# Strassen products of a hybrid encoder step: A21 and A22 of the next job loaded ahead of A12, low parts issued behind the eviction, S3 behind the second product's low part

## The chip, the cores and the metric

The kernel runs on one core of one Trainium2 chip. The metric is the device time of one launch in microseconds, the median of three runs; a profiled execution of the same program gives the trace that is read here.

## The reference, cut to what matters

One step of an encoder layer over 576 frames (512 of a prompt, 64 of a running stream), model width 2048, inner width 5504, all in fp32:

```python
h = x + jnp.concatenate([oa, ob], axis=-1) @ w_out        # oa: attention heads, ob: gated MLP groups
n = rms_norm(h, g)
a, gv = jnp.split(n @ w_up, 2, axis=-1)
ac, new_prev = causal_dwconv(prev, a, cw, cb)
y = h + (jax.nn.silu(ac) * gv) @ w_down
```

What goes before (RMS norm, the products of w_in, chunked attention, spatial gating) takes the first 609 us of the span and is not touched by the change.

## The kernel before

Each fp32 product is made of three products in a rounded type. A weight tile w is split into hi (a rounded copy) and lo = w - hi, and so is the activation, into u0 and u1. TensorE then adds hi x u0, hi x u1 and lo x u0 in one PSUM bank. The hi part of a tile is a cast on ScalarE (L216), the lo part a subtraction on VectorE (L217); both are made by `split_raw`. All weights come from DRAM through the helper `load_raw` (L206), whose transfers are issued by SyncE (SP in the profile).

From w_out on the products are done by 2x2 blocks with seven products in place of eight (Strassen in Winograd's form). The program is a list of jobs: 12 jobs of the out product (o0 to o11), 40 of the up product (u3 to u42) and 29 of the down product (d0 to d28). A job has a pair of output tiles and a window of units; a unit is a 256-row piece of the contraction. All up jobs have 8 units. Out jobs have 1 to 8 and down jobs 1 to 8, since their contraction is cut into visits: near the ends of both stages the windows are short and change from job to job.

A job needs four weight blocks A11, A12, A21 and A22, of one 128x128 tile per unit each (512 KB at 8 units). On VectorE the sums S1 = A21 + A22 (L875), S3 = A11 - A21 (L878, into A21's buffer), S2 = S1 - A11 (L879, into A11's) and T = A12 - S2 (L882, into A12's) are made of them. The seven products go in the order 1, 2, 6, 5, 7, 3, 4; their weights are A11, A12, S2, S1, S3, T and A22. Their results are added in three PSUM banks: x takes products 1, 6, 7 and 4, one after another, y product 2, z products 5 and 3. So product 6 must not start before product 1 has been evicted from x. The activation sums (units un_c, un_n, un_f) are made beside, in the out and down stages by VectorE and ScalarE while the jobs run (`form`).

The main loop, for product i of the whole list, does `prep(i + 1)` (sums, split and the loads for the next job), `mm(i)`, `evict(i - 1)`, `finish(i - 3)` and `form`. The tool that builds the program orders the instructions of each engine anew, by its own model of when each is ready; the orders shown below are those that it gave. The pool of weight buffers (tag raw) has five: four blocks and S1. A block of the next job takes the buffer that was given back first, and its transfer waits on SP until the lo part that last read the buffer is done. In the kernel before the next job's A11 takes the old A11's buffer, A12 the one of S1 (free behind lo_5), A21 that of A21 (behind lo_7), A22 that of A12 (behind lo_3), and the new S1 that of A22.

The matmuls are at L909 (hi x u0), L911 (hi x u1) and L913 (lo x u0), the evictions of out and down jobs at L979 (one addition into the residual tiles r0, r1, or y), those of up jobs at L940 to L962. Residual tiles are loaded at L865, and stored at L985 and L694. The activations of the up product go to DRAM at L999 (ac) and come back as fa and fb (L791) for the down product's units (L543, L546, L567, L568).

Of the kernel before, what the change touches and what calls it, by code (L numbers as in the profile page):

```python
# [9 lines left out]
F32R = mybir.dt.float32r  # L10
AF = mybir.ActivationFunctionType
ALU = mybir.AluOpType
# [3 lines left out]
P = 128  # L16
# [109 lines left out]
def layer(ctx: ExitStack, tc: tile.TileContext, xT, xg0, wst, cst, strip, ckT, cv, gws, cstate,  # L126
          yT, kTo, vTo, convo, gvo, stream):
    nc = tc.nc
    const = ctx.enter_context(tc.tile_pool(name="const", bufs=1))
    wpool = ctx.enter_context(tc.tile_pool(name="wpool", bufs=3))  # L130
# [32 lines left out]
    def big(name):  # L163
        return tmpp.tile([P, 640], F32, tag="tmp", name=name)
# [30 lines left out]
    def f(ap):  # L195
        return ap.bitcast(F32)
# [3 lines left out]
    def load_raw(keys, name):  # L200
        raw = wpool.tile([P, 8 * P], F32, tag="raw", name=f"raw_{name}", bufs=5)
        w = len(keys) * P
        src = wst[woff[0]:woff[0] + P * w].rearrange("(p c) -> p c", p=P)
        woff[0] += P * w
        stream.append(keys)
        nc.sync.dma_start(raw[:, :w], src)  # L206
        return raw

    def split_raw(raw, n, name, fast=False):
        hi = wpool.tile([P, 8 * P], F32R, tag="hi", name=f"hi_{name}", bufs=2)  # L210
        lo = wpool.tile([P, 8 * P], F32R, tag="lo", name=f"lo_{name}", bufs=2)
        w = n * P
        if fast:
            nc.vector.tensor_copy(hi[:, :w], raw[:, :w])
        else:
            nc.scalar.copy(hi[:, :w], raw[:, :w])  # L216
        nc.vector.tensor_tensor(lo[:, :w], raw[:, :w], f(hi[:, :w]), ALU.subtract)  # L217
        return hi, lo
# [612 lines left out]
    def strassen(jobs):  # L831


        work = [(job, r) for job in jobs for r in ORDER]
        R, PSX, EV, HL, RES = {}, {}, {}, {}, {}
        tt = nc.vector.tensor_tensor

        def window(job):
            return range(HP) if job[0] == UP else range(*PLANS[job[0]][job[1]][1:3])

        def single(job):

            return job[0] == DOWN and PLAN[job[1]][1] == 0

        def extra(job, r):
            return 1 if single(job) and r in (2, 3, 4) else 0

        def load(job, q):
            mi, half = int(q[0]) - 1, int(q[1]) - 1
            if job[0] == UP:  # L850
                keys = [(("ag"[mi], job[1]), 2 * i + half) for i in window(job)]
            else:
                m = (job[0], 2 * PLANS[job[0]][job[1]][0] + mi)
                keys = [(m, 2 * p + half + (job[0] == DOWN)) for p in window(job)]
                if single(job) and half:
                    keys.append((m, 0))
            R[job, q] = load_raw(keys, f"{job[0]}{job[1]}_{q}")

        def load_res(job):
            if job[0] != UP:  # L860
                i, lo = PLANS[job[0]][job[1]][:2]
                RES[job] = [big(f"r{c}_{job[0]}{job[1]}")[:, :T] for c in range(2)]
                first, later = (hs, ys) if job[0] == DOWN else (xT, hs)
                for c in range(2):
                    nc.sync.dma_start(RES[job][c], (later if lo else first)[2 * i + c])  # L865

        def prep(i):
            if i >= len(work):
                return
            job, r = work[i]  # L870
            name = f"{job[0]}{job[1]}"
            w = len(window(job)) * P
            if r == 2:
                R[job, "s1"] = wpool.tile([P, 8 * P], F32, tag="raw", name=f"s1_{name}", bufs=5)
                tt(R[job, "s1"][:, :w], R[job, "21"][:, :w], R[job, "22"][:, :w], ALU.add)  # L875
            elif r == 6:
                a11, a21 = R[job, "11"][:, :w], R[job, "21"][:, :w]
                tt(a21, a11, a21, ALU.subtract)  # L878
                tt(a11, R[job, "s1"][:, :w], a11, ALU.subtract)  # L879
            elif r == 5:  # L880
                a12 = R[job, "12"][:, :w]
                tt(a12, a12, R[job, "11"][:, :w], ALU.subtract)  # L882
            q = {1: "11", 2: "12", 6: "11", 5: "s1", 7: "21", 3: "12", 4: "22"}[r]
            HL[job, r] = split_raw(R[job, q], len(window(job)) + extra(job, r), f"{r}_{name}")
            nxt = {5: "11", 7: "12", 3: "21", 4: "22"}.get(r)
            at = i // len(ORDER) + 1
            if nxt and at < len(jobs):
                load(jobs[at], nxt)
                if r == 4:
                    load_res(jobs[at])  # L890

        def operand(job, k, r):
            return UN[UNITS[job[0]], k, r][0]
# [42 lines left out]
        def evict_up(j, r, ps):  # L936
            x, y, z = ps
            if r == 1:
                EV[j] = {"cc": big(f"cc_{j}")[:, :T]}
                nc.scalar.copy(EV[j]["cc"][:, LEFT], x)  # L940
            ev = EV[j]
            if r == 2:
                ev["e"] = e = conv_edges(j)
                tt(e[:, 2:2 + HF], y, ev["cc"][:, LEFT], ALU.add)
            elif r == 6:
                nc.scalar.copy(ev["cc"][:, RIGHT], x)
            elif r == 5:
                ev["act"] = big(f"act_{j}")[:, :T]
                nc.scalar.copy(ev["act"][:, RIGHT], z)
            elif r == 7:  # L950
                tt(ev["act"][:, RIGHT], x, ev["act"][:, RIGHT], ALU.add)
            elif r == 3:
                e, cc, m = ev["e"], ev["cc"], SEQ - HF
                tt(e[:, 2 + HF:514], z[:, :m], cc[:, HF:SEQ], ALU.add)  # L954
                tt(e[:, 516:580], z[:, m:], cc[:, SEQ:], ALU.add)
                ev["t"] = conv(j, e)
            elif r == 4:
                t, act = ev["t"], ev["act"]
                nc.scalar.activation(t, t, AF.Silu)
                tt(act[:, HF:SEQ], act[:, HF:SEQ], t[:, HF:SEQ], ALU.mult)  # L960
                tt(act[:, SEQ:], act[:, SEQ:], t[:, 514:578], ALU.mult)
                tt(act[:, :HF], x, t[:, :HF], ALU.mult)  # L962

        def evict_sum(job, r, ps):
            x, y, z = ps[:3]
            rs = RES[job]
            i, _, hi, _ = PLANS[job[0]][job[1]]
            src, m, c = {1: (x, 0, LEFT), 2: (y, 0, LEFT), 6: (x, 0, RIGHT), 5: (z, 1, RIGHT),
                         7: (x, 1, RIGHT), 3: (z, 0, RIGHT), 4: (x, 1, LEFT)}[r]
            dst = rs[m]  # L970
            end = job[0] == OUT and hi == HP
            if end and r in (2, 3, 7, 4):
                k = 2 * i + m
                if Y[k] is None:
                    Y[k], Y_SLOT[k] = slot([P, T], F32, f"y_{k}")
                dst = Y[k]
            if r == 4 and len(ps) == 4:
                tt(rs[1][:, RIGHT], ps[3], rs[1][:, RIGHT], ALU.add)
            tt(dst[:, c], src, rs[m][:, c], ALU.add)  # L979
            if r in (3, 4):  # L980
                if end:
                    out_done(2 * i + m)
                else:
                    out = hs if job[0] == OUT else yT if hi == NP else ys
                    nc.sync.dma_start(out[2 * i + m], rs[m])  # L985

        def evict(i):
            if 0 <= i < len(work):
                job, r = work[i]
                if job[0] == UP:  # L990
                    evict_up(job[1], r, PSX[job])
                else:
                    evict_sum(job, r, PSX[job])

        def finish(i):
            if 0 <= i < len(work):
                job, r = work[i]
                if r == 4 and job[0] == UP:
                    nc.sync.dma_start(acs[job[1]], EV.pop(job[1])["act"])  # L999
                    if job[1] == NF - 1:  # L1000
                        nc.sync.dma_start(convo, conv_new)
# [10 lines left out]
        def form(job):  # L1012
            return limit(job) and advance(step, forming, limit(job))

        for q in ("11", "12", "21", "22"):
            load(jobs[0], q)
        load_res(jobs[0])
        prep(0)
        for i in range(len(work)):
            prep(i + 1)  # L1020
            mm(i)
            evict(i - 1)
            finish(i - 3)
            form(work[i][0])
            if work[i][1] == ORDER[-1]:
                while form(work[i][0]):
                    pass
        evict(len(work) - 1)

    flush()  # L1030
    banks(misc=8)
    strassen([(OUT, v) for v in range(len(PLAN_O))])
    for _ in rms_scale(rx, "h"):
        pass
# [91 lines left out]
```

## Time and profile before

| | |
|---|---|
| median of three runs | 2320.21 us (2320.01 to 2320.77) |
| the profiled execution | 2321.35 us |
| its span, first to last instruction | 2319.6 us |
| TensorE busy | 2250.9 us, 97%, 16768 matmuls |
| VectorE busy | 1694.7 us, 73% |
| ScalarE busy | 1003.5 us, 43% |
| GpSimd busy | 207.8 us, 9% |
| DRAM traffic | 286 MB, 123 GB/s |

TensorE is in the rows as PE, its weight loads as PEld, VectorE as DVE, ScalarE as ACT, GpSimd as POOL and SyncE's queue as SPq. A row of the trace with a bracket at its end gives the idle time of the engine ahead of the instruction and what ended it. Names of tiles are given without the job's number: x_o is the x bank of an out job, hi_d the hi part of a down job. The stages in the trace: heads and gated MLP to 609 us, out jobs to 816, norm and the first up products to 915, up jobs to 1803, down jobs to 2320.

### The profile page before, as it was taken

What the parts mean: (1) busy time and instruction counts of PE and PEld (TensorE: products, weight loads), DVE (VectorE), ACT (ScalarE), POOL (GpSimd) and SP (SyncE); (2) the same over time, 40 slices, a digit from 0 to 9 for tenths busy, and PEclk for the clock granted to TensorE, in tenths of its full rate; (3) what the DMA queues carried; (4) which work ended last, traced back from release to release, by engine and by line L of the source; (5) the groups of instructions that cost most, each with busy time, mean ns of one, the idle gap of its engine ahead of it and who ended that gap; (6) DMA issues with size and microseconds to landing.
All of it is one profiled execution on the core that took longest, in us unless ns stands there. A gap on an engine that the chain in (4) does not pass through costs nothing.

```text
span 2319.6 us, 41325 instructions
## 1 busy us (share of the span) xinstructions
PE 2250.9 (97%) x16768; PEld 2233.3 (96%) x16768; DVE 1694.7 (73%) x2605; ACT 1003.5 (43%) x1485; POOL 207.8 (9%) x242
## 2 busy tenths in 40 slices
PE   7999999999999889999999999999999899999988
PEld 7999999999999779999999999999999899999988
DVE  7645655654787669777777777677777999978767
ACT  5444444432433345444444444444445444434332
POOL 4000000000002102111111111111111000000000
PEclk9999999999999889999999999999999999999999
DMA  6322222222344332333332333323333665545444
GB/s 211 102 92 92 97 94 80 83 84 78 119 152 138 127 103 92 103 125 105 104 117 93 123 106 103 120 91 122 107 102 123 210 195 173 188 161 179 157 146 141
DMA packets 107391, 286.24 MB, mean 123 GB/s; under 512 B 12096, under 2 KB 20416, under 8 KB 107200
## 3 DMA queue, kind: packets, MB, share of 16 engines
q1 hardware_dynamic: 107200, 283.60, 37.2%
q8 instruction: 132, 2.16, 0.4%
q14 instruction: 59, 0.48, 0.1%
HBM read 241.62 MB, written 41.93 MB: 122 GB/s over the span
## 4 chain that ended last, share of the span: by engine, by line
PE 64%; DVE 4%; DMA 2%; ACT 1%; issue 1%; POOL 0%; SPq 0%; ACTq 0%; DVEq 0%; POOLq 0%
PE x_u L911 7%; PE x_u L909 7%; PE x_u L913 7%; PE z_u L911 4%; PE z_u L909 4%; PE z_u L913 4%; PE x_d L909 3%; PE x_d L911 3%; PE x_d L913 3%; PE y_u L913 2%; PE y_u L911 2%; PE y_u L909 2%; PE ps_a L238 2%; PE z_d L909 2%; PE z_d L911 2%; PE z_d L913 2%
## 5 line engine op out<-in xcount | busy, mean ns | idle before, releaser
L216 ACT CAST hi_u<-raw_u 128x1024 fp32r<-128x1024 f32 x256 | 269.0, 1051 | 502.9 <-PE x_u L911 280.0
L217 DVE TENSOR_TENSOR lo_u<-raw_u,hi_u 128x1024 fp32r<-128x1024 f32 x256 | 312.9, 1222 | 223.0 <-ACT hi_u L216 222.5
L911 PE MATMUL x_u<-un_n,hi_u 128*128 128x288 f32 x1280 | 344.7, 296 | 0.0
L909 PE MATMUL x_u<-un_n,hi_u 128*128 128x288 f32 x1280 | 344.5, 295 | 0.0
L216 ACT CAST hi_d<-raw_d 128x896 fp32r<-128x896 f32 (+7 forms) x174 | 144.0, 828 | 249.0 <-PE x_d L911 104.7
L909 PEld LDWEIGHTS x_u<-un_n,hi_u 128*128 128x128 f32 x1280 | 242.1, 189 | 0.0
L911 PEld LDWEIGHTS x_u<-un_n,hi_u 128*128 128x128 f32 x1280 | 240.1, 188 | 0.0
L909 PE MATMUL x_d<-un_f,hi_d 128*128 128x288 f32 x672 | 185.5, 301 | 18.8 <-ACT hi_d L216 11.8
L913 PE MATMUL x_u<-un_n,lo_u 128*128 128x288 f32 x1280 | 195.2, 295 | 0.0
L911 PE MATMUL x_d<-un_f,hi_d 128*128 128x288 f32 x672 | 182.3, 296 | 0.0
L913 PEld LDWEIGHTS x_u<-un_n,lo_u 128*128 128x128 f32 x1280 | 178.4, 188 | 0.0
L217 DVE TENSOR_TENSOR lo_d<-raw_d,hi_d 128x896 fp32r<-128x896 f32 (+7 forms) x174 | 164.0, 943 | 17.5 <-ACT hi_d L216 16.4
L911 PE MATMUL z_u<-un_n,hi_u 128*128 128x288 f32 x640 | 172.2, 296 | 0.0
L909 PE MATMUL z_u<-un_n,hi_u 128*128 128x288 f32 x640 | 171.8, 295 | 0.0
L909 PEld LDWEIGHTS x_d<-un_f,hi_d 128*128 128x128 f32 x672 | 127.2, 189 | 25.1 <-ACT hi_d L216 19.8
L911 PEld LDWEIGHTS x_d<-un_f,hi_d 128*128 128x128 f32 x672 | 127.1, 189 | 0.0
L751 POOL COPY conv_new<-e 128x2 f32<-128x2 f32 x43 | 51.9, 1208 | 827.1 <-DVE e L954 766.3
L909 PEld LDWEIGHTS z_u<-un_n,hi_u 128*128 128x128 f32 x640 | 120.3, 188 | 0.0
L911 PEld LDWEIGHTS z_u<-un_n,hi_u 128*128 128x128 f32 x640 | 120.3, 188 | 0.0
L913 PE MATMUL x_d<-un_f,lo_d 128*128 128x288 f32 x672 | 108.3, 296 | 0.0
L216 ACT CAST hi_o<-raw_o 128x1024 fp32r<-128x1024 f32 (+7 forms) x72 | 54.9, 764 | 116.2 <-PE x_o L911 44.8
L913 PE MATMUL z_u<-un_n,lo_u 128*128 128x288 f32 x640 | 97.3, 294 | 0.0
(361 smaller groups left out, 5776.8 us busy)
## 6 DMA issues: line engine op xcount, KB each, us to landing
raw_u<-wst SPq DMA_DIRECT2D x176, 512.0 KB, 3.7
raw_d<-wst SPq DMA_DIRECT2D x56, 448.0 KB, 3.6
ac<-act SPq DMA_DIRECT2D x43, 288.0 KB, 3.6
ys<-r_d SPq DMA_DIRECT2D x42, 288.0 KB, 2.5
r_d<-ys SPq DMA_DIRECT2D x42, 288.0 KB, 3.1
raw_b<-wst SPq DMA_DIRECT2D x16, 512.0 KB, 3.2
raw_o<-wst SPq DMA_DIRECT2D x16, 512.0 KB, 3.6
raw_v<-wst SPq DMA_DIRECT2D x14, 512.0 KB, 3.2
```

Of the source, the lines that this page charges most:

```text
L216: nc.scalar.copy(hi[:, :w], raw[:, :w])
L217: nc.vector.tensor_tensor(lo[:, :w], raw[:, :w], f(hi[:, :w]), ALU.subtract)
L238: nc.tensor.matmul(out, w, x[j] if isinstance(x, tuple) else x[:, j * HF:(j + 1) * HF], start=st, stop=sp)
L751: nc.gpsimd.tensor_copy(conv_new[:, j, 0:2], e[:, 512:514])
L909: nc.tensor.matmul(out, w, u[:, 0], start=first and k == 0, stop=False, skip_group_check=True)
L911: nc.tensor.matmul(out, w, u[:, 1], start=False, stop=False, skip_group_check=True)
L913: nc.tensor.matmul(out, lo[:, k * P:(k + 1) * P], u[:, 0], start=False, stop=not add and k == n - 1, skip_group_check=True)
```

## The change

Three things change in `strassen`. First, the next job's loads are issued in another order: A11 and A21 with product 5, A22 with product 7, A12 with product 3 (A11 with 5, A12 with 7, A21 with 3 and A22 with 4 before). Going by the buffers of the built program A21 now takes S1's buffer, A22 that of A21, and A12 its own. The very first job's order stays. Second, `split_raw` is taken apart: `prep` makes only the hi part, and a new function `low` makes the lo part, called behind the eviction. Third, S3 moves from ahead of S2 to behind the lo part of product 2.

```diff
--- before.py
+++ after.py
@@ -205,6 +205,16 @@
         stream.append(keys)
         nc.sync.dma_start(raw[:, :w], src)
         return raw
+
+    def high_raw(raw, n, name):
+        hi = wpool.tile([P, 8 * P], F32R, tag="hi", name=f"hi_{name}", bufs=2)
+        nc.scalar.copy(hi[:, :n * P], raw[:, :n * P])
+        return hi
+
+    def low_raw(raw, hi, n, name):
+        lo = wpool.tile([P, 8 * P], F32R, tag="lo", name=f"lo_{name}", bufs=2)
+        nc.vector.tensor_tensor(lo[:, :n * P], raw[:, :n * P], f(hi[:, :n * P]), ALU.subtract)
+        return lo
 
     def split_raw(raw, n, name, fast=False):
         hi = wpool.tile([P, 8 * P], F32R, tag="hi", name=f"hi_{name}", bufs=2)
@@ -874,20 +884,33 @@
                 R[job, "s1"] = wpool.tile([P, 8 * P], F32, tag="raw", name=f"s1_{name}", bufs=5)
                 tt(R[job, "s1"][:, :w], R[job, "21"][:, :w], R[job, "22"][:, :w], ALU.add)
             elif r == 6:
-                a11, a21 = R[job, "11"][:, :w], R[job, "21"][:, :w]
-                tt(a21, a11, a21, ALU.subtract)
+                a11 = R[job, "11"][:, :w]
                 tt(a11, R[job, "s1"][:, :w], a11, ALU.subtract)
             elif r == 5:
                 a12 = R[job, "12"][:, :w]
                 tt(a12, a12, R[job, "11"][:, :w], ALU.subtract)
             q = {1: "11", 2: "12", 6: "11", 5: "s1", 7: "21", 3: "12", 4: "22"}[r]
-            HL[job, r] = split_raw(R[job, q], len(window(job)) + extra(job, r), f"{r}_{name}")
-            nxt = {5: "11", 7: "12", 3: "21", 4: "22"}.get(r)
+            n = len(window(job)) + extra(job, r)
+            hi = high_raw(R[job, q], n, f"{r}_{name}")
+            HL[job, r] = R[job, q], hi, n, f"{r}_{name}"
             at = i // len(ORDER) + 1
-            if nxt and at < len(jobs):
-                load(jobs[at], nxt)
+            if at < len(jobs):
+                for nxt in {5: ("11", "21"), 7: ("22",), 3: ("12",)}.get(r, ()):
+                    load(jobs[at], nxt)
                 if r == 4:
                     load_res(jobs[at])
+
+        def low(i):
+
+            if i >= len(work):
+                return
+            job, r = work[i]
+            raw, hi, n, name = HL[job, r]
+            HL[job, r] = hi, low_raw(raw, hi, n, name)
+            if r == 2:
+                w = len(window(job)) * P
+                a21 = R[job, "21"][:, :w]
+                tt(a21, R[job, "11"][:, :w], a21, ALU.subtract)
 
         def operand(job, k, r):
             return UN[UNITS[job[0]], k, r][0]
@@ -1016,10 +1039,12 @@
             load(jobs[0], q)
         load_res(jobs[0])
         prep(0)
+        low(0)
         for i in range(len(work)):
             prep(i + 1)
             mm(i)
             evict(i - 1)
+            low(i + 1)
             finish(i - 3)
             form(work[i][0])
             if work[i][1] == ORDER[-1]:
```

What the built order makes of it, on three engines. VectorE in out job o4, around the eviction of product 1 from x (r_o<-x_o); the lo part with hi_o_7491 is that of product 6. Before:

```order
L879 TENSOR_TENSOR raw_o_11_7303<-s_o_7454,raw_o_11_7303 128x1024
L882 TENSOR_TENSOR raw_o_12_7333<-raw_o_12_7333,raw_o_11_7303 128x1024
L217 TENSOR_TENSOR lo_o_7492<-raw_o_11_7303,hi_o_7491 128x1024
L979 TENSOR_TENSOR r_o_7401<-x_o_7460,r_o_7401 128x288
L217 TENSOR_TENSOR lo_o_7522<-s_o_7454,hi_o_7521 128x1024
L979 TENSOR_TENSOR y_7551<-y_o_7461,r_o_7401 128x288
```

After:

```order
L216 TENSOR_TENSOR lo_o_7487<-raw_o_12_7368,hi_o_7456 128x1024
L891 TENSOR_TENSOR raw_o_12_7368<-raw_o_12_7368,raw_o_11_7301 128x1024
L1002 TENSOR_TENSOR r_o_7399<-x_o_7458,r_o_7399 128x288
L216 TENSOR_TENSOR lo_o_7518<-raw_o_11_7301,hi_o_7491 128x1024
L1002 TENSOR_TENSOR y_7551<-y_o_7459,r_o_7399 128x288
L216 TENSOR_TENSOR lo_o_7553<-s_o_7454,hi_o_7521 128x1024
```

The eviction of product 1 now stands ahead of the lo part of product 6, and so on down the job. S2 (L888, not in the second piece) stands just ahead of lo_2 there.

SP's queue in the up stage, the loads of one job (u20) and the store of the job ahead. Before:

```order
L206 DMA raw_u_11_13682<-wst 128x1024
L999 DMA ac_6603<-act_13539 128x576
L206 DMA raw_u_12_13717<-wst 128x1024
L206 DMA raw_u_21_13748<-wst 128x1024
L206 DMA raw_u_22_13780<-wst 128x1024
```

After:

```order
L1022 DMA ac_6603<-act_13539 128x576
L206 DMA raw_u_11_13680<-wst 128x1024
L206 DMA raw_u_21_13682<-wst 128x1024
L206 DMA raw_u_22_13717<-wst 128x1024
L206 DMA raw_u_12_13748<-wst 128x1024
```

A12 is now the last of the four, and the store stands ahead of A11 instead of behind it.

ScalarE in the down job d1: casts of its own weights (raw_d_11 and s_d, the fifth and sixth rows, are those of products 6 and 5) and of the down product's units (un_f). Before:

```order
L216 CAST hi_d_19443<-raw_d_11_19374 128x384
L216 CAST hi_d_19463<-raw_d_12_19391 128x512
L543 CAST un_f_1_19649<-fa_19489 128x288
L543 CAST un_f_3_19653<-fb_19490 128x288
L216 CAST hi_d_19495<-raw_d_11_19374 128x384
L216 CAST hi_d_19520<-s_d_19461 128x384
```

After:

```order
L211 CAST hi_d_19463<-raw_d_12_19411 128x512
L553 CAST un_f_1_19650<-fa_19490 128x288
L211 CAST hi_d_19495<-raw_d_11_19372 128x384
L211 CAST hi_d_19520<-s_d_19461 128x384
L553 CAST un_f_7_19517<-acc 128x288
L553 CAST un_f_3_19654<-fb_19491 128x288
```

The casts for products 6 and 5 now stand ahead of the cast of fb, which a transfer from DRAM delivers. In out job o8 (and o10) SP's queue also has r0, a residual tile, ahead of A11, where it stood behind A22 (A12).

## Rows read from the trace of the kernel before

**Rows 1.** Busy time by stretch: TensorE, weight loads, VectorE, ScalarE, GpSimd; clock, DMA share, GB/s.
```profile
1000.00:1800.00 800.00, 800.00 (x6040) 800.00 (x6040) 593.99 (x739) 363.11 (x448) 112.09 (x144) 1.00 0.33 109
...
792.00:797.20 5.20, 4.95 (x20) 4.95 (x21) 2.29 (x6) 1.64 (x4) 0.00 (x0) 0.50 0.36 115
```

**Rows 2.** TensorE's waits, whole span: engine line <- releaser: us, times, longest.
```profile
PE x_o L909 <- ACT hi_o L216: 13.0, 7, 5.1
PE x_d L909 <- ACT hi_d L216: 11.8, 10, 2.5
...
PE x_d L909 <- DVE r_d L979: 6.4, 8, 1.3
...
PE x_o L909 <- DVE r_o L979: 4.0, 5, 1.6
```

**Rows 3.** TensorE's waits for evictions, 609 to 700 us and 2000 to 2220 us.
```profile
PE x_o L909 <- DVE r_o L979: 2.1, 3, 1.2
...
PE x_d L909 <- DVE r_d L979: 1.5, 3, 0.7
```

**Rows 4.** Timeline of out job o4: start, us, engine, line, out<-in, count, idle and releaser.
```profile
679.47 1.05 ACT L216 CAST hi_o<-raw_o 128x1024 fp32r<-128x1024 f32 x1 [4.53 <-DVE raw_o L879]
...
679.89 1.21 PE L913 MATMUL y_o<-un_c,lo_o 128*128 128x288 f32 x8
...
680.56 1.23 DVE L217 TENSOR_TENSOR lo_o<-raw_o,hi_o 128x1024 fp32r<-128x1024 f32 x1
681.70 0.45 DVE L979 TENSOR_TENSOR r_o<-x_o,r_o 128x288 f32<-128x288 f32 x1
...
682.30 0.37 PE L909 MATMUL x_o<-un_c,hi_o 128*128 128x288 f32 x1 [1.20 <-DVE r_o L979]
```

**Rows 5.** Timeline, TensorE: first matmuls of products in the down jobs that waited.
```profile
1809.33 0.37 PE L909 MATMUL x_d<-un_f,hi_d 128*128 128x288 f32 x1 [1.30 <-DVE r_d L979]
...
1835.57 0.38 PE L909 MATMUL x_d<-un_f,hi_d 128*128 128x288 f32 x1 [0.93 <-DVE r_d L979]
...
1852.07 0.37 PE L909 MATMUL x_d<-un_f,hi_d 128*128 128x288 f32 x1 [0.88 <-DVE r_d L979]
...
1947.59 0.37 PE L909 MATMUL x_d<-un_f,hi_d 128*128 128x288 f32 x1 [0.87 <-DVE r_d L979]
...
2118.66 0.37 PE L909 MATMUL x_d<-un_f,hi_d 128*128 128x288 f32 x1 [1.15 <-ACT hi_d L216]
...
2152.80 0.37 PE L909 MATMUL x_d<-un_f,hi_d 128*128 128x288 f32 x1 [0.58 <-ACT hi_d L216]
```

**Rows 6.** Timeline of jobs o8, o10 and d1, around the start of product 6.
```profile
760.28 0.61 PE L909 MATMUL x_o<-un_c,hi_o 128*128 128x288 f32 x1 [2.84 <-ACT hi_o L216]
...
789.59 0.56 DVE L875 TENSOR_TENSOR s_o<-raw_o,raw_o 128x384 f32<-128x384 f32 x1 [3.17 <-DMA raw_o<-wst]
...
792.25 0.61 PE L909 MATMUL x_o<-un_c,hi_o 128*128 128x288 f32 x1 [5.13 <-ACT hi_o L216]
...
1816.24 0.55 DVE L879 TENSOR_TENSOR raw_d<-s_d,raw_d 128x384 f32<-128x384 f32 x1
...
1817.11 0.43 ACT L543 CAST un_f<-fb 128x288 fp32r<-128x288 f32 x1 [2.42 <-DMA fb<-ac]
...
1818.01 0.40 PE L909 MATMUL x_d<-un_f,hi_d 128*128 128x288 f32 x1 [1.40 <-ACT hi_d L216]
```

**Rows 7.** Timeline of an up job: SP's late loads, and hi_2 of the next job.
```profile
1210.16 6.71 SPq L206 DMA_DIRECT2D raw_u<-wst  x3
...
1223.68 1.06 ACT L216 CAST hi_u<-raw_u 128x1024 fp32r<-128x1024 f32 x1 [2.13 <-PE x_u L911]
```

**Rows 8.** Page, DMA issues: tiles, queue, count, KB each, us from issue to landing.
```profile
raw_u<-wst SPq DMA_DIRECT2D x176, 512.0 KB, 3.7
```

**Rows 9.** Timeline of down job d25, around the start of product 2.
```profile
2263.43 0.29 PE L909 MATMUL y_d<-un_f,hi_d 128*128 128x288 f32 x1
2263.45 0.96 DVE L875 TENSOR_TENSOR s_d<-raw_d,raw_d 128x768 f32<-128x768 f32 x1
```

## The prediction

> **What bounds the kernel now.** I read the busy time by stretch first, to see where TensorE has room at all. In the stretch from 1000 to 1800 us, which is 36 jobs of the up product (168 matmuls each), it is busy 800.00 of 800 us with 6040 matmuls, 132.5 ns each [rows 1]: there nothing that VectorE or the loads do in another order can be worth anything, it can only hurt. Then the waits of TensorE over the whole span [rows 2]: the first matmul of a product (L909) waits for two things only. Either the hi cast of its weights on ScalarE is late (13.0 us in the out jobs, 11.8 in the down jobs), or VectorE has not yet evicted the PSUM bank x that the product writes (L979: 4.0 and 6.4 us). Together 35.2 us, 1.5% of the span: that is all that this change can reach, and nearly all of it lies in jobs that are short or whose neighbours have another length.
>
> **Why the evictions are late, and what the change does to them.** One place shows the pattern [rows 4]. In out job o4 product 6 can't start because x still holds product 1. The matmuls of product 1 were over before those of product 2 began; product 2's last eight start at 679.89. VectorE, however, takes lo_6 first (680.56, 1.23 us), and the eviction only at 681.70; TensorE stands from the end of product 2 to 682.30, 1.20 us. The lo part is not wanted until two thirds of product 6 are through, about 2 us after its start, the eviction at once. The change exchanges the two, and the order of the new program says that it really does (the first piece of order above). The eviction would then begin at about 680.6, end at 681.05, and product 6 could follow its predecessor without a gap (hi_6, cast from 679.47 on in 1.05 us, was done). The lo follows at 681.0 to 682.2, with product 6's third pass due at 683.2: covered. If it weren't, the third pass would wait for that difference.
>
> Sum of this part, place by place. In 609 to 700 us three such waits make 2.1 us [rows 3], all with nothing but a lo ahead of the eviction: taken whole, 2.1. In 2000 to 2220 us three make 1.5 [rows 3], the same pattern: 1.5. At 1947.59 (0.87) and 2152.80 (0.58) the eviction also stands right behind lo_6 [rows 5]; the second is put down to the cast, which ended at about the same time as the eviction, so I take both whole with a floor of 0 on the second: 1.45. At 1809.33, 1835.57, 1852.07 and 2118.66 (1.30, 0.93, 0.88, 1.15) the eviction stands behind the lo too, but there VectorE and ScalarE also turn out the down product's operands (un_f) just before, and these are next late. I take 0.4, 0.5, 0.65 and 0.5, near the lo's own duration for the first three (2, 4 and 5 units, at 0.15 us a unit by the 1.23 us for eight of [rows 4]) and half of it for the last (7 units); together 2.05, between 0 and 4.26. Sum: 7.1 us, bounds 4.5 and 9.3. The waits of this kind between 700 and 800 us, 1.9 us of [rows 2]'s 4.0, I count at nothing: just behind them product 1 of the next job waits for its block A11 from DRAM, and takes up what is won.
>
> **The loads.** SP's four waits per job are the same as before, only the blocks change places: A21 comes where A12 came, A22 where A21 came, A12 last. S1 = A21 + A22 can so start one landing earlier, and with it S2 and hi_6. In the three out and down jobs where hi_6 is the late one [rows 6]: at 760.28 (2.84 waited) A22 lands one block of 512 KB earlier, but lo_2 now lies between S3 and S2, and the load of r0, 288 KB, has been put ahead of A11; I take 0.4. At 792.25 (5.13 waited) S1 starts at 789.59, when the last of four small blocks has landed; now it starts one block earlier and product 2, with its block last, fills part of the wait: 0.9. At 1818.01 (1.40) ScalarE stood in front of a cast that waits for a transfer (un_f<-fb, 1817.11, 2.42 idle) while S2 (L879, 1816.24, 0.55 us) was done by 1816.8, and hi_6 came behind it; in the new order hi_6 and hi_5 stand ahead of that cast: 0.8. Four more such waits, the last jobs of the down product, I count at nothing: there lo_2, which must have A12, stands ahead of S2, so that what S1 gains A12 gives back; one of them, the last job, may lose 0.2. Sum: 1.9 us (0.4 + 0.9 + 0.8 - 0.2); bounds -1.0, if r0's transfer costs o8's first product 0.8 and nothing else is won, and 4.7, half of what the three waits hold.
>
> In the up jobs the loads cost nothing: the last of the three late issues leaves SP by 1216.9 [rows 7], a block lands 3.7 us after its issue [rows 8], at 1220.6, and hi_2 starts at 1223.68, held there by TensorE's release of the hi buffer (2.13) and not by data [rows 7]: A12, now in that slot, has 3 us of cover. Gone, it would cost what is missing, once per job. The store of act is now behind A12's issue, and nobody waits for it in the next job. S3 is meant to move behind lo_2; in most jobs the new order still has S3 right behind S1, so this part I count at nothing.
>
> **The sum.** 7.1 + 1.9 = 9.0 us off the profiled execution's 2321.35 gives 2312.4 us; the median of the runs is 1.14 us lower than that execution, so 2320.2 - 9.0 = **2311.2 us**. With both bounds: 14.0 us and 3.5 us, 2306.2 to 2316.7.
>
> [...] [Rows 4] show an eviction whose operand had been ready for over 3 us and which was held by nothing but the lo ahead of it. [...]
>
> **The rivals.** *Given back (0.24).* In the new order lo_(i+1) can start only when product i-1 has ended and been evicted, 0.45 us, and takes 0.15 us per unit of eight [rows 4]; product i and two thirds of i+1 last 0.66 us per unit. From two units on the lo is in time, in jobs of one unit (o7, d22) it is late by about 0.3 us in each of seven products: 4.6 us. With that the time is 2315.8. The same end is reached if the waits for the evictions merely turn into waits for hi casts, which stand close behind (at 2152.80 the two ended together [rows 5]): if half of the 9.0 comes back, 2315.7; if all, 2320.2. I put this case at 2315.6 to 2320.5. Against it: most of the rows name VectorE alone as what came last, and in [rows 4] the hi cast had been done for over a microsecond and a half.
>
> *Slower (0.07).* A12 last. In the job of [rows 9] product 2 starts at 2263.43, and S1, which needs the block that lands last, at 2263.45: with A12 in that slot, hi_2 (some 0.8 us for six units, by the 1.05 for eight of [rows 4]) starts then and product 2 stands that long. In seven jobs (o8, o10, o11, d23, d25, d27, d28) loads are that late. A stand can also bring TensorE's clock to half: after the 5.13 us wait it was granted 0.50 over 792.0 to 797.2 us, 20 matmuls in 4.95 us of busy time where they take 2.65 [rows 1], 2.3 us lost; smaller waits cost about 1.7 on the estimate that the loss goes on for three quarters as long. At all seven 7 x 2.5 = 17.5 us: 2328.7. From four places on (10 us) it outweighs the 9.0. Against it: what product 2 waits for, product 6 then has in advance, since S1 is earlier by one block.
>
> *More (0.12).* If the wait at 760.28 closes altogether (2.4 beyond the 0.4), that at 792.25 is halved (1.7 beyond the 0.9), and the stretch at half clock behind it doesn't come (2.3): 6.4 more, 2304.8. Against it: S2 still has S1, S3 and lo_2 ahead of it.
>
> *It doesn't do what it says (0.02).* If S1's earlier start is lost altogether because S3 still stands ahead of S2, the 1.9 goes: 2313.1, still faster.
>
> **How the numbers follow.** The forecast has 0.55, its own range 2306.2 to 2315.6. A measurement of this kernel can tell about 0.2% or 4.6 us from no change, so faster means under 2315.6: the forecast, "more" and "doesn't do" give 0.69; "given back" is the same, 0.24; slower 0.07. The range leaves out the slower case, the uppermost part of "given back" and the lowest of "more": 2303.5 to 2319.0.
>
> **What would show it.** Right: TensorE's waits for L979's successor fall from 10.4 us to under 3; the wait at 682.30 is gone and product 6 of o4 starts within 0.1 us of product 2's end; 1000 to 1800 us still has 800 of 800 busy; the wait of 5.13 us in o10 is near 4. Wrong: new waits of the third pass (L913's successor) for lo parts in one-unit jobs would show the first rival; waits of the y bank's first matmul, product 2, for hi at job starts the second. Any idle time of TensorE in the up jobs would overthrow the whole working, since 40 jobs would multiply it: 0.25 us in each are 10 us.

## The result, and the profile after

The changed kernel takes 2305.28 us (median of 4 runs, 2303.89 to 2307.83) where the kernel before takes 2320.26 (4 runs). The ratio is 0.9936, 95% interval 0.9919 to 0.9954. That is 15.0 us less, where 9.0 were forecast; it lies inside the range of 2303.5 to 2319.0, on the side of the third rival ("more").

The first row is the page's busy time of the changed kernel; the others are TensorE's waits over its whole span, largest of the block products first (columns as in [rows 2]). L932 is the first matmul of a product and L936 its third pass, L909 and L913 before; L1002 is the eviction.

```profile
PE 2244.4 (97%) x16768; PEld 2229.9 (97%) x16768; DVE 1703.2 (74%) x2605; ACT 998.2 (43%) x1485; POOL 211.4 (9%) x242
```
```profile
PE x_d L932 <- ACT hi_d L211: 9.7, 10, 3.0
...
PE x_o L932 <- ACT hi_o L211: 6.8, 6, 2.7
...
PE y_d L932 <- ACT hi_d L211: 3.3, 3, 1.6
...
PE y_o L932 <- ACT hi_o L211: 2.7, 1, 2.7
PE z_d L936 <- DVE lo_d L216: 1.3, 1, 1.3
PE y_o L936 <- DVE lo_o L216: 1.0, 2, 0.7
...
PE z_o L936 <- DVE lo_o L216: 0.9, 1, 0.9
...
PE x_d L932 <- DVE r_d L1002: 0.4, 1, 0.4
```

The waits for evictions, 10.4 us in [rows 2], are down to 0.4. The waits of x banks for hi casts fell from 24.8 to 16.5 us; new ones have come, 6.0 us for the hi cast of product 2 (y_d, y_o) and 4.6 us for low parts (L936, the two smallest left out above). The up jobs took 890.34 us from the first matmul of the first to that of the first down job, and take 890.34 now: the loads' new order costs nothing there, as forecast from [rows 7].

By stage, from first matmul to first matmul in the two profiled executions: out jobs 210.99 to 204.38 us (6.6 less), norm and first up products 92.38 to 90.71, up jobs the same, down jobs (to the last matmul) 512.33 to 503.34 (9.0 less). The 1.7 us in the norm stage are not put down to the change: the kernel before ran there at half clock in one more place (granted 0.50 over 886.2 to 889.2 us), and two further profiles of the changed kernel show 93.68 and 90.75 us for that stage.

### The profile page after: what moved, and what is told of

Same layout as the page of the kernel before. It is cut to its first block, busy times and chain, and to the rows that moved or that the text cites. A ratio compares the mean times of both kernels' runs of the same rounds, so it can differ in the third digit from the quotient of the medians.

```text
span 2302.2 us, 41222 instructions
## 1 busy us (share of the span) xinstructions
PE 2244.4 (97%) x16768; PEld 2229.9 (97%) x16768; DVE 1703.2 (74%) x2605; ACT 998.2 (43%) x1485; POOL 211.4 (9%) x242
## 4 chain that ended last, share of the span: by engine, by line
PE 92%; DVE 4%; DMA 2%; issue 1%; ACT 1%; SPq 0%; POOL 0%; ACTq 0%; DVEq 0%; POOLq 0%
PE x_u L934 7%; PE x_u L932 7%; PE x_u L936 7%; PE ps_u L248 4%; PE ps_b L248 4%; PE ps_q L248 4%; PE ps_k L248 4%; PE ps_v L248 4%; PE z_u L934 4%; PE z_u L932 4%; PE z_u L936 4%; PE x_d L932 4%; PE x_d L934 4%; PE x_d L936 3%; PE y_u L936 2%; PE y_u L934 2%
## 5 line engine op out<-in xcount | busy, mean ns | idle before, releaser
L216 DVE TENSOR_TENSOR lo_u<-raw_u,hi_u 128x1024 fp32r<-128x1024 f32 x240 | 292.8, 1220 | 136.4 <-ACT hi_u L211 136.4
L211 ACT CAST hi_u<-raw_u 128x1024 fp32r<-128x1024 f32 x240 | 250.6, 1044 | 302.4 <-PE z_u L934 149.6
L932 PE MATMUL x_u<-un_n,hi_u 128*128 128x288 f32 x1280 | 344.5, 295 | 0.0
L932 PEld LDWEIGHTS x_u<-un_n,hi_u 128*128 128x128 f32 x1280 | 242.1, 189 | 0.0
L936 PE MATMUL x_u<-un_n,lo_u 128*128 128x288 f32 x1280 | 195.2, 295 | 0.0
L932 PE MATMUL x_d<-un_f,hi_d 128*128 128x288 f32 x672 | 184.4, 299 | 10.2 <-ACT hi_d L211 9.7
L936 PEld LDWEIGHTS x_u<-un_n,lo_u 128*128 128x128 f32 x1280 | 178.4, 188 | 0.0
L932 PE MATMUL z_u<-un_n,hi_u 128*128 128x288 f32 x640 | 171.8, 295 | 0.0
L932 PEld LDWEIGHTS x_d<-un_f,hi_d 128*128 128x128 f32 x672 | 127.2, 189 | 13.9 <-ACT hi_d L211 13.1
L932 PEld LDWEIGHTS z_u<-un_n,hi_u 128*128 128x128 f32 x640 | 120.3, 188 | 0.0
L936 PE MATMUL x_d<-un_f,lo_d 128*128 128x288 f32 x672 | 107.7, 295 | 0.0
L936 PE MATMUL z_u<-un_n,lo_u 128*128 128x288 f32 x640 | 97.3, 294 | 0.0
```

The costliest lines, as they stand in the source:

```text
L211: nc.scalar.copy(hi[:, :n * P], raw[:, :n * P])
L216: nc.vector.tensor_tensor(lo[:, :n * P], raw[:, :n * P], f(hi[:, :n * P]), ALU.subtract)
L932: nc.tensor.matmul(out, w, u[:, 0], start=first and k == 0, stop=False, skip_group_check=True)
L936: nc.tensor.matmul(out, lo[:, k * P:(k + 1) * P], u[:, 0], start=False, stop=not add and k == n - 1, skip_group_check=True)
```

## The experiments

Two theories stood at the start. **E**, the prediction's: evictions are late since a low part stands ahead of them on VectorE, so the new order of the two gives most. **L**: the load order gives most. The first four runs do one part of the change each, or move A12.

**Low part behind the eviction, alone** (edit of the kernel before).

```diff
-            HL[job, r] = split_raw(R[job, q], len(window(job)) + extra(job, r), f"{r}_{name}")
+            hi = high_raw(R[job, q], n, f"{r}_{name}")
...
             evict(i - 1)
+            low(i + 1)
```

> The kernel before with one part of the change: the low part is issued behind the eviction; loads in the old order (A11, A12, A21, A22), S3 ahead of S2 as before. Theory E (the eviction order gives most): all waits in which an eviction stood behind a lo part close, in o0, o1, o4, d0, d2, d8, d11, d13, d14, d16 and d18, 9 to 10 us, so about 2310.5 us; the waits of product 6 for its hi cast in o8 and o10 (2.84 and 5.13 us) stay. Theory L (the load order gives most, since VectorE no longer stands in S1's wait for A22 with evictions queued behind it): under 4 us gained, 2316 us or more.

**Loads in the new order, alone** (edit of the kernel before).

```diff
-            nxt = {5: "11", 7: "12", 3: "21", 4: "22"}.get(r)
+                for nxt in {5: ("11", "21"), 7: ("22",), 3: ("12",)}.get(r, ()):
```

> The kernel before with one part of the change: the next job's loads in the order A11, A21, A22, A12; low part ahead of the eviction as before. Theory E: the waits behind lo parts stay (o4 still 1.20 us), o8, o10, d23 and d28 get shorter by some 4 to 5 us together, so about 2315.5 us. Theory L: 2308 to 2310 us, and the waits for evictions at L979 fall well under 10.4 us.

**S3 behind product 2's low part, alone** (edit of the kernel before).

```diff
             elif r == 6:
-                tt(a21, a11, a21, ALU.subtract)
...
             HL[job, r] = split_raw(R[job, q], len(window(job)) + extra(job, r), f"{r}_{name}")
+            if r == 2:
+                tt(a21, R[job, "11"][:, :w], a21, ALU.subtract)
```

> The kernel before with one part of the change: S3 behind product 2's low part in program order, nothing else. Both theories: the built order differs from that of before in a few rows only, within 1 us of before, 2319.5 to 2321.

**A12 third, A22 last** (edit of the changed kernel).

```diff
-                for nxt in {5: ("11", "21"), 7: ("22",), 3: ("12",)}.get(r, ()):
+                for nxt in {5: ("11", "21"), 7: ("12",), 3: ("22",)}.get(r, ()):
```

> The changed kernel with A12 loaded ahead of A22 (A11, A21, A12, A22). If what the changed kernel still loses is A12's late landing, the waits of product 2 (2.7 us in o10, 3.3 us in down jobs) close and S1's stay covered: 2301 to 2303 us. If S1's start is what counts at the ragged jobs, product 6 waits for its hi cast by as much again or more, as it did before: 2305 to 2309 us.

Measured, each against the kernel before on the same chip (its median there 2322.4 us):

| kernel | median us | ratio | 95% interval |
|---|---|---|---|
| low part behind the eviction alone | 2316.3 | 0.9972 | 0.9959 to 0.9986 |
| loads in the new order alone | 2308.4 | 0.9938 | 0.9923 to 0.9953 |
| S3 alone | 2321.0 | 0.9991 | 0.9979 to 1.0004 |
| A12 third, A22 last (all else as changed) | 2321.6 | 0.9991 | 0.9981 to 1.0000 |

E falls. The loads alone give the gain of the whole change, as L expected, and the waits for evictions fall to 6.8 us with them; E expected some 2315.5 us there. The eviction order alone gives 6.1 us, less than half; that lies between the two expectations (9 to 10, and under 4) and decides nothing. With A22 last again the whole change is worth nothing that can be told from zero. There both expectations (2301 to 2309 us) missed by more than 12 us; x banks wait 27.0 us for hi casts, where they waited 24.8 before:

```profile
PE x_d L932 <- ACT hi_d L211: 16.2, 13, 2.8
PE x_o L932 <- ACT hi_o L211: 10.8, 7, 3.1
```

Why that kernel is by the medians also 5 us behind the eviction order alone is open. S3 alone does nothing that can be told from zero; with the other two parts in place it does not even alter the built program: with S3 put back ahead of S2 the order of every engine is the same, row for row.

Which waits closed shows in the jobs' times, from the first matmul of a job to that of the next, as differences to before in us:

| job | the wait before | changed | loads alone | evictions alone | A12 third |
|---|---|---|---|---|---|
| o0 | eviction of 6, 0.39 | -0.89 | 0.00 | -0.84 | -0.89 |
| o4 | eviction of 1, 1.20 | -1.44 | -1.44 | -1.44 | -1.44 |
| o8 | hi_6, 2.84 | -1.29 | -2.83 | +1.32 | +1.76 |
| o10 | hi_6, 5.13 | -2.50 | -2.26 | -1.64 | -2.12 |
| d0 | eviction of 6, 1.30 | -0.88 | +0.01 | -0.68 | -0.93 |
| d1 | hi_6, 1.40 | -0.57 | -0.77 | +3.15 | +2.42 |
| d8 | eviction of 1, 0.87 | -1.05 | -1.05 | -1.05 | -1.05 |
| d11 | eviction of 1, 0.70 | -1.23 | -1.23 | -0.27 | +0.29 |
| d13 | eviction of 1, 0.25 | -0.49 | -0.49 | +0.59 | +0.50 |
| d16 | eviction of 6, 1.15 | -1.49 | -0.51 | -1.49 | -1.53 |
| d18 | eviction of 1, 0.58 | -0.81 | -0.81 | -0.51 | -0.15 |
| d25 | hi_6, 1.65 | +0.57 | -0.59 | +1.82 | +1.74 |

There are two kinds of late eviction. That of product 6 (o0, d0, d16) needs the new order of eviction and low part. That of product 1 (o4, d8, d11, d13, d18) closes with the loads alone, although in o4 the low part of product 6 still stands ahead of it. VectorE's timeline of o4 tells why, first of the kernel before, where S1 is L875:

```profile
672.87 1.23 DVE L875 TENSOR_TENSOR s_o<-raw_o,raw_o 128x1024 f32<-128x1024 f32 x1 [2.14 <-DMA raw_o<-wst]
```

and with the loads alone:

```profile
670.33 1.22 DVE L875 TENSOR_TENSOR s_o<-raw_o,raw_o 128x1024 f32<-128x1024 f32 x1
...
678.00 1.22 DVE L217 TENSOR_TENSOR lo_o<-raw_o,hi_o 128x1024 fp32r<-128x1024 f32 x1
679.14 0.45 DVE L979 TENSOR_TENSOR r_o<-x_o,r_o 128x288 f32<-128x288 f32 x1
...
680.50 0.29 PE L909 MATMUL x_o<-un_c,hi_o 128*128 128x288 f32 x1
```

Before, VectorE had stood 2.14 us in front of S1, since A22, the last block, had not landed; everything behind it in its queue, S3, lo_2, S2, T, lo_6 and at the end the eviction of [rows 4], was late by that. With A22 a slot earlier S1 has no wait, the same chain ends 2.56 us earlier (679.14 against 681.70; 0.45 of that is an earlier start of the job), and product 6 starts at 680.50 right behind product 2. So the wait of o4 had two conditions, the late chain and the lo part ahead of the eviction: taking away either closes it, as the table shows, and the prediction saw only the second. In d11, d13 and d18 the eviction order alone does not close the wait, the loads do.

VectorE's waits for S1's blocks over the whole span, one row of each kernel: before, changed, evictions alone, loads alone, A12 third.

```profile
DVE s_d L875 <- DMA raw_d<-wst: 14.9, 20, 1.6
```
```profile
DVE s_d L885 <- DMA raw_d<-wst: 3.5, 5, 1.4
```
```profile
DVE s_d L885 <- DMA raw_d<-wst: 20.2, 18, 2.1
```
```profile
DVE s_d L875 <- DMA raw_d<-wst: 2.5, 3, 1.4
```
```profile
DVE s_d L885 <- DMA raw_d<-wst: 14.0, 12, 2.0
```

The kernels in which this wait is short gain most; it does not order the others, since the eviction order alone has the longest (20.2) and gains 6.1 us. And a load order changes more than S1's wait, what lies on SP's queue and in the DMA engines at a time, and which buffers are given back when. So theory **S** (VectorE's stand in S1's wait makes the rest late) was put against a rival **T** (the order of the transfers as such), with an edit of the kernel before that takes the wait away and moves no load: its S1 leaves A22 out.

```diff
-                tt(R[job, "s1"][:, :w], R[job, "21"][:, :w], R[job, "22"][:, :w], ALU.add)
+                tt(R[job, "s1"][:, :w], R[job, "21"][:, :w], R[job, "12"][:, :w], ALU.add)
```

> The kernel before, but S1 is made of A21 and A12 in place of A21 and A22, so that the results of products 2 to 7 are not the reference's; loads in the old order, low parts ahead of the evictions. It takes away S1's wait for the block that lands last and moves no load. Theory S (VectorE's stand in S1's wait is what makes evictions and hi_6 late): the wait of product 6 in o4 closes, those in d8, d11, d13, d14 and d18 too, about 2308 us as with the new load order alone. Rival T (the order of the transfers as such, what SP's queue and the DMA engines do at a time): stays at 2318 us or more, and o4's 1.20 us wait stays.

It took 2307.5 us, ratio 0.9935 (0.9921 to 0.9948). VectorE's waits and o4's timeline:

```profile
DVE s_d L875 <- DMA raw_d<-wst: 0.5, 1, 0.5
```
```profile
669.84 1.22 DVE L875 TENSOR_TENSOR s_o<-raw_o,raw_o 128x1024 f32<-128x1024 f32 x1
...
678.64 0.46 DVE L979 TENSOR_TENSOR r_o<-x_o,r_o 128x288 f32<-128x288 f32 x1
```

Its jobs o4, d8, d11, d13, d14 and d18 are shorter by the same 1.44, 1.05, 1.23, 0.49, 0.70 and 0.81 us as with the loads alone. T falls, S stands.

**What the eviction order adds.** The changed kernel and the loads alone were then run side by side, and with them a mixture (an edit of the changed kernel) that takes the new order only where the first kind of late eviction needs it, that of product 6.

> The changed kernel once more, beside the next two on the same chip: 2304 to 2308 us.

> The new load order alone once more, to weigh it against the whole change. If the two parts heal the same waits, it lies 0 to 4 us above the changed kernel; if they add up, 6 us or more above.

```diff
+            if i + 1 < len(work) and work[i + 1][1] != 7:
+                low(i + 1)
             mm(i)
             evict(i - 1)
-            low(i + 1)
+            if i + 1 < len(work) and work[i + 1][1] == 7:
+                low(i + 1)
```

> The changed kernel with the low part behind the eviction for product 7 alone (there the eviction of product 6 frees x for product 7), ahead of it for the others. What the new load order alone still loses to evictions are the waits between product 5 and product 7 in o0, o1, o7, d0, d2, d3, d16 and d22, 6.8 us; what the changed kernel loses by evictions ahead of low parts are waits for low parts in o7, o8, d0 and d23, some 4.6 us. If these two go together, 2302 to 2304 us; if the first come back as waits for hi casts, the same as the changed kernel.

Changed 2304.9 us, 0.9924 (0.9911 to 0.9938); loads alone 2308.6, 0.9943 (0.9930 to 0.9955); the mixture 2308.1, 0.9936 (0.9923 to 0.9948). The medians put the eviction order at 3.7 us on top of the loads, against the 6.1 us that it gives alone; the intervals overlap, so its size on top is open. The mixture missed both of its expectations (2302 to 2304 us, or the same as the changed kernel) and is the same as the loads alone: d16 gained 1.05, where the loads alone gained 0.51 in their first profile and 1.20 in their second, and d0 gained nothing, since there product 7 still waits for that eviction. TensorE's waits in 1797 to 1808 us of the mixture:

```profile
PE x_d L932 <- DVE r_d L1002: 1.0, 1, 1.0
```

**Short jobs.** In the first profiles the changed kernel loses against the loads alone in o8 and d25, both behind a job of one or two units. A last edit of the changed kernel puts the low part ahead of the eviction again in short jobs.

```diff
+            if first(i + 1):
+                low(i + 1)
             mm(i)
             evict(i - 1)
-            low(i + 1)
+            if not first(i + 1):
+                low(i + 1)
...
+            return len(window(job)) <= 3 and not (job[0] == DOWN and job[1] < 2)
```

> The changed kernel with the low part ahead of the eviction again in the short jobs (windows of up to 3 units, but not the first two down jobs): o7, o9, o10, d22, d24 and d26. There the low part is what gives back a buffer, on which a load of the next job waits, and the changed kernel lost in o7, o8, d24 and d25 what the new load order alone had won (o8 1.3 against 2.8 us, d25 0.6 lost against 0.6 won). If that is the cause, o8 and d25 win about 2 us together: 2302.5 to 2304.5 us. If not, the same as the changed kernel, 2304 to 2307 us.

> The changed kernel beside it on the same chip: 2304 to 2307 us.

2305.5 us, 0.9930 (0.9915 to 0.9945), beside 2306.0, 0.9935 (0.9922 to 0.9949), for the changed kernel: the same. o8 did win (2.83 us shorter than before, as with the loads alone), but o10 gave it back (1.12 shorter, against 2.5 in the changed kernel), and d25 was 0.56 longer than before, where the changed kernel's three profiles show 0.57, 1.01 and 2.09. The loads alone, 0.59 shorter there at first, were 2.50 longer in their second profile: d25 tells executions apart, not kernels. No version beat the changed kernel by more than the runs differ.

## Why the prediction was right or wrong

**What bounds, and where there is room: right.** The up jobs moved by nothing, and the gain lies in the out and down jobs, where the waits of [rows 2] stood.

**Late evictions: right that they close, half of the cause, and too small.** The first step read [rows 4] one link back: the eviction stood behind lo_6, and "nothing but a lo" held it. The row of S1 above, 9 us earlier on the same queue, was not followed. For the eviction of product 1 VectorE's stand in front of A22 was needed too, and in d11, d13 and d18 the exchange alone did not close the wait; for that of product 6 in o0 and d0 the forecast's cause holds. This decided nothing about the sign, since the change heals both. But by the working's terms the eviction order alone was worth 7.1 us and the loads alone 1.9. Measured by the medians they gave 6.1 (with d13 not closed and d1, o8 and d25 longer than before) and 14.0, in the second run 14.7: the forecast put the larger part of the gain in the wrong half of the change. The size: the places counted at 7.1 us became shorter by 9.5 (o0, o1 and o4 by 3.0 for 2.1; d8 and d18 by 1.9 for 1.45; d11, d13 and d14 by 2.4 for 1.5; d0, d2, d3 and d16 by 2.2 for 2.05).

**The price of a wait.** The working took the idle time of a row as its worth. In the places where the wait went clean away it was 0.23 us more: o4, d8, d13, d14, d16 and d18 waited 4.57 us by the rows and became shorter by 5.98 (d11, 0.70 and 1.23, had a second, shorter stand and is left out). In [rows 4] the last of product 2's eight begins at 679.89 + 1.21 - 0.29 = 680.81, and product 6 at 682.30, 1.49 us later, where 0.13 us is the pace of [rows 1]: 1.36 and not 1.20, as a row's idle time starts at the modelled end of the last matmul. The first matmul behind the wait then takes 0.37 us, while without one (680.50 above) it takes 0.29: together the 1.44 that o4 became shorter.

**The loads: sign right, size wrong.** 1.9 us were forecast; o8, o10, d1 and the last seven down jobs became shorter by 1.3, 2.5, 0.6 and 1.5, 5.8 in all. In the next two profiles of the changed kernel the four sum to 6.0 and 2.6; d1 was 0.8 and 0.1 longer there, so its term is not shown. o10 is the term that failed most (0.9 forecast, 2.5 to 2.8 in all three). The first matmul of its product 2 in the changed kernel:

```profile
784.75 0.40 PE L932 MATMUL y_o<-un_c,hi_o 128*128 128x288 f32 x1 [2.73 <-ACT hi_o L211]
```

S1 now has no wait at all (its row, at 781.33, is in the last section), where [rows 6] show 3.17 us; product 2 now waits 2.73 for A12, as the slower rival said, but product 6 not at all, where it waited 5.13 (the forecast looked for some 4 there). The forecast gave the earlier S1 the length of one block's transfer. What it gives is the whole chain of S1, S3, S2 and the cast, which now runs while product 2 waits. The last down jobs were counted at nothing for the same reason (d23 and d28 each gained 0.9 in two profiles, 0.2 in the third).

**700 to 800 us.** The waits for evictions there were counted at nothing; o7 in fact lost 0.7 us (0.3 and 0.0 in the next two profiles). Its third pass waited 0.9 for a low part (z_o L936 <- lo_o above), but not as the first rival has it: that low part took 1.23 us, where one of its size takes 0.28, beside an addition on GpSimd.

```profile
740.38 0.28 DVE L216 TENSOR_TENSOR lo_o<-raw_o,hi_o 128x128 fp32r<-128x128 f32 x1
...
740.82 1.41 POOL L710 TENSOR_TENSOR acc<-acc,sqy 128x576 f32<-128x576 f32 x1 [1.80 <-ACT sqy L709]
...
741.14 1.23 DVE L216 TENSOR_TENSOR lo_o<-s_o,hi_o 128x128 fp32r<-128x128 f32 x1
```

**Given back.** The rival's sign came, 4.6 us of waits for low parts where the kernel before has 0.2, but in six products (o7, o8, o9, o10, d0, d23), not in the fourteen of o7 and d22; that its price was 4.6 too is chance. An eviction that is not ready and holds up the low part behind it stands in o8 (2.32 us for its residual tile) and d23 (1.27 us for its product).

**S3: right,** it counts nothing. **The up jobs' cover: right.**

**The slower rival** had the mechanism (product 2 waits for A12, 6.0 us in the changed kernel) and the sign of its sum wrong. A12 third and A22 last, the kernel with little of that wait (1.0 us), is 0.9991 of the kernel before: x banks then wait those 27.0 us for hi casts. **More** named 2304.8, and 2305.3 was measured, but that is luck: it has 4.9 us for o10 (wait and clock) and 2.8 for o8, which became 2.5 and 1.3 shorter. The rest came from places that it does not name.

**The 17.4 us** by which the two profiled executions differ in span hold 1.7 us of the norm stage, which differs by 3 us between executions of the changed kernel; the medians' 15.0 is the figure to hold against 9.0. The places above sum to 9.5 + 5.8 - 0.7, d9 and o11 hold 0.7 more, and what is left is spread in parts of under 0.2.

**VectorE's queue** reaches further than the prediction took it: the eviction in [rows 4] was held up not by lo_6 alone but first by S1, nine instructions ahead in the same queue (672.87 and 681.70, and no row between shows idle time). With S1 2.54 us earlier, by the loads alone, that eviction came 2.56 us earlier.

## What to carry to other kernels

When an engine delivers late, as VectorE did in o4 (the eviction nine instructions behind S1's stand of 2.14 us), go back along its own queue to where it last stood idle; the instruction just ahead of the late one may only be the last of a late chain. In a pipeline of loads, ask how much work hangs on a block, and not only which block the next product takes first: here the block that starts the longest chain (A22, for S1) had to come earlier, and the one that the next product wants first (A12) could come last. Two edits that close the same wait don't add up, so each is to be run alone before the gain is put down to one of them.

## What the runs showed of the hardware

Some waits of a microsecond or two were followed by a stretch in which TensorE's granted clock was 0.50, so that the place lost more than the wait itself. In the run with the eviction order alone, d1 waited 1.05 and 1.69 us for VectorE and ScalarE, and then ran with 0.50 granted:

```profile
1816.50:1822.30 5.80, 5.80 (x25) 5.80 (x25) 4.05 (x11) 1.15 (x3) 0.00 (x0) 0.50 0.71 215
```

25 matmuls in 5.80 us, 2.5 us more than at 0.1325 us each; the job became 3.2 us longer. No run shows what lowers the clock. An estimate of what such stretches cost behind 600 us (three matmuls or more in a row that start 0.20 to 0.26 us apart, where this stretch has 0.23 and that of [rows 1] 0.25, less 0.1325 us each): 13 us in the kernel before, 8, 10 and 11 in the changed kernel's three profiles, 10 and 15 in the loads alone, 17 in the eviction order alone, 16 with A12 third. The mean granted clock of these executions was 0.990, then 0.992, 0.991 and 0.991, 0.991 and 0.990, 0.987, and 0.988. By the estimate the same program differs by 3 to 5 us from one execution to the next in this way, which is why differences below that were left open; and by this estimate 2 to 5 us of the change's gain may be clock that fell less often, against a single profile of the kernel before.

In o10 S1 took 1.81 us in the changed kernel and 0.56 before [rows 6], on the same 128x384. GpSimd was adding beside it:

```profile
781.31 3.08 POOL L710 TENSOR_TENSOR acc<-acc,sqy 128x576 f32<-128x576 f32 x2 [4.69 <-ACT sqy L709]
781.33 1.81 DVE L885 TENSOR_TENSOR s_o<-raw_o,raw_o 128x384 f32<-128x384 f32 x1
...
783.17 1.63 DVE L913 TENSOR_TENSOR raw_o<-raw_o,raw_o 128x384 f32<-128x384 f32 x1
```

An S1 that starts earlier can so also run into work that was over before: in the kernel before GpSimd's two additions there lay at 785.75 to 788.66, and S1 began at 789.59. Behind 600 us of the changed kernel's trace 11 of VectorE's additions and subtractions of two SBUF tiles took 0.3 to 1.3 us longer than others of their shape, and all 11 began while GpSimd added. The 8 that began before such an addition and ran into it kept their time within 0.01 us, and so did the evictions that began while GpSimd added, 2 here and 6 in the kernel before, which have one input in PSUM. No run took GpSimd's addition away; the cause rests on this comparison.
